# How the weight parts of a ConvGLU up projection lie in SBUF: steps of 8 and 16 elements, or side by side with a shift

## Chip, cores and metric

The kernel runs on one core of one Trainium2 chip. The metric is device time of one execution in microseconds.

## What is computed

One layer of a hybrid encoder block in float32 on 512 tokens of width 1024: an RMSNorm, a wide input projection, three token mixers (a bidirectional mLSTM, a 2-D neighbourhood attention, a cross-attention into 256 memory tokens), a gated merge and an output projection; then a feed-forward network with a convolution and a gate, and a last RMSNorm. Cut to what matters here:

```python
D_MODEL, SEQ, D_FF = 1024, 512, 2816

def conv_glu_ffn(h, w_up, w_conv, b_conv, w_down):
    a, u = jnp.split(h @ w_up, 2, axis=-1)
    return (jax.nn.gelu(dwconv3(a, w_conv, b_conv)) * u) @ w_down

def reference(...):
    h = rms_norm(x, mix_norm_g[l])
    proj = h @ w_in[l]
    ...                      # the three mixers y_ml, y_na, y_xa and their gates
    merged = g_ml * (y_ml @ w_br_ml[l]) + g_na * (y_na @ w_br_na[l]) + g_xa * (y_xa @ w_br_xa[l])
    x = x + merged @ w_out[l]
    x = x + conv_glu_ffn(rms_norm(x, ffn_norm_g[l]), w_ffn_up[l], w_ffn_conv[l], b_ffn_conv[l], w_ffn_down[l])
    return rms_norm(x, final_norm_g)
```

The change is in the product `h @ w_up`. It is 1056 of the kernel's matmuls.

## The kernel before

**Three matmuls for one product.** Each operand is split into a high part of type float32r (a rounded copy) and a low part (the rest). `mm3` (L228 to L231) then issues high x high (L229), high x low (L230) and low x high (L231) into the same PSUM tile. The weights are the stationary operand: each matmul has a weight load of its own (PEld), 128 columns of 128 partitions, and streams 512 tokens past it.

**Weight blocks.** All weights stand in `wflat` in HBM, cut into blocks in the order of use (`BLOCKS`). A block of the up projections, `("ua", f)` for the part that goes through the convolution and `("uu", f)` for the gate, has 8 slices of 128 x 128 (one for each 128 of the 1024 inputs), so 1024 elements on each partition and 24 matmuls. There are 22 tiles f of 128 hidden features, taken in two passes `hh` of 11, and a pass runs `ua 0, uu 0, ua 1, uu 1, ...` and then its half of the down projection (`dn` blocks of 11 slices, 33 matmuls for each of the output tiles).

**From HBM to the array.** `weights(key)` is called when a block is needed. It issues the DMA of blocks up to three ahead (`emit_raw`, L153, three `raw` buffers) and the split of the block one ahead (`emit_split`). The split works in two halves of 4 slices, 512 columns each: ScalarE copies the high part (L213, or L207 where the step is 4), VectorE subtracts for the low part (L214 or L208). Each half goes to a buffer `w` of 1088 elements a partition, of which there are four, so two blocks. A `w` buffer is free again when PE has read it.

**Layouts.** `FORMS` gives for each up block a triple: a step, a shift and a direction; `layout` takes them in turn, 22 of them, so each form is used once in each pass. With step 1, the high part lies at the shift and the low part 512 elements behind it. With step 2, high and low elements alternate, so a weight load reads every second element. With step 4, two slices' high and low elements alternate and a load reads every fourth. Where the direction is 1, `proj` (L360) streams the tokens backwards. All other blocks lie side by side at shift 0.

**The order of work.** The program is written in the order of the model; a scheduler then fixes an order for each engine, and each engine keeps to its own. In the feed-forward part, a tile f needs: the `ua` product in PSUM, the factor `rb2` of the norm, a chain `pad` (L398, VectorE), three taps (L400 ScalarE, L401 and L402 VectorE), the gelu (L1167 ScalarE, L1168 VectorE, L1169 ScalarE, L1170 VectorE), a product with `rb2` on POOL (L1171), the product with the `uu` result (L1174, VectorE) and a split (L235 ScalarE, L236 VectorE) into the hidden activation. For f = 0, `ua` and `uu` are run up to the last slice, then the sums of the norm (L311) go through PE; `ua 1` follows, and only behind it `rstd_row` makes `rb2` (L329 on PE, L331 on ScalarE). PSUM has four banks `mm` for these products.

**Buffers.** The pool `up` has 15 buffers `unit` of 2112 elements a partition. In the feed-forward part, two hold the residual stream, four the normed input, six the hidden activation of a pass.

Of the kernel before, what the change touches and what calls it, by code (L numbers as in the profile page):

```python
# [11 lines left out]
F32 = mybir.dt.float32  # L12
# [5 lines left out]
P = 128  # L18
# [35 lines left out]
def block_list():  # L54
# [50 lines left out]
def hybrid_block(ctx, tc, xT, memT, wflat, vecs, gbias, nabias, outa, outb):  # L105
# [14 lines left out]
    def nm(s):  # L120
        uid[0] += 1
        return f"{s}_{uid[0]}"
# [38 lines left out]
    def layout(key):  # L161

        if key[0] in ("ua", "uu"):
            return FORMS[(2 * key[1] + (key[0] == "uu")) % len(FORMS)]
        return 1, 0, 0

    def form(w, step, at, m, c):

        if step == 2:
            e = w[:, at:at + 2 * m].rearrange("p (j x) -> p x j", x=2)  # L170
            h, l = e[:, 0, :], e[:, 1, :]
        elif step == 4:
            e = w[:, at:at + 2 * m].rearrange("p (y j z x) -> p x y z j", y=2, x=2, z=2)
            h, l = e[:, 0], e[:, 1]
            return h, l, [(h[:, k // 2, k % 2], l[:, k // 2, k % 2]) for k in range(4)]
        else:
            h, l = w[:, at:at + m], w[:, WT - m:] if m > 512 else w[:, 512 + at:512 + at + m]
        q = [slice(k * c, (k + 1) * c) for k in range(m // c)]
        return h, l, [(h[:, s], l[:, s]) for s in q]

# [9 lines left out]
    def emit_split(i):  # L190
        key, n = BLOCKS[i]
        r = raws.pop(i)
        c, hs = halves(i)
        split[i] = []
        for a, b in hs:
            m = (b - a) * c
            if key[0] == "dnl":
                h, l = lastw(4 * key[1] + a, m)
                parts = [(h[:, k * c:(k + 1) * c], l[:, k * c:(k + 1) * c]) for k in range(b - a)]
            else:  # L200
                step, at, _ = layout(key)
                w = wp.tile([P, WT], F32R, tag="w", name=nm("w"), bufs=4)
                h, l, parts = form(w, step, at, m, c)
            for u, v in ((0, P), (P, m)) if i == 0 and a == 0 else ((0, m),):
                src = r[:, a * c + u:a * c + v]
                if len(h.shape) == 4:
                    A.activation(h, src.rearrange("p (y z j) -> p y z j", y=2, z=2), AF.Copy)  # L207
                    V.tensor_tensor(l, src.rearrange("p (y z j) -> p y z j", y=2, z=2), h.bitcast(F32), op=ALU.subtract)  # L208
                    continue
                if i == 0 and a == u == 0:  # L210
                    V.tensor_copy(h[:, u:v], src)
                else:
                    A.activation(h[:, u:v], src, AF.Copy)  # L213
                V.tensor_tensor(l[:, u:v], src, h[:, u:v].bitcast(F32), op=ALU.subtract)  # L214
            split[i].extend(parts)
# [144 lines left out]
    def proj(key, XHs, XLs, n=S, bank=None, at={}):  # L360
        ws = weights(key)
        ps = (bank or mmps)()
        for k in range(KT):
            if layout(key)[2]:
                mm3(ps[:, ::-1], ws[k][0], ws[k][1], XHs[k][:, ::-1], XLs[k][:, ::-1], k == 0, k == KT - 1)
            else:
# [832 lines left out]
def _layout(inp):  # L1199
# [14 lines left out]
    for key, n in BLOCKS:  # L1214
# [39 lines left out]

# [43 lines left out]
```

## Time and profile before

| | |
|---|---|
| median of two runs | 898.5 us (897.97 and 899.04) |
| the profiled execution | 899.35 us |
| its span, first to last instruction | 897.6 us |
| granted TensorE clock, mean | 0.999 |
| PE busy | 888.7 us, 99% |
| PEld (weight loads) busy | 758.9 us, 85% |
| VectorE (DVE) busy | 599.7 us, 67% |
| ScalarE (ACT) busy | 467.6 us, 52% |
| POOL busy | 158.0 us, 18% |
| HBM read | 94.67 MB, 110 GB/s over the span |

PE stands for TensorE's matmuls, PEld for the weight loads, which lie beside matmuls. The profile gives a start and a duration for each instruction; a matmul's end is modelled, so the distance between starts says more than the duration. A row of a group reads: line, engine, operation, output<-inputs, shapes, count | busy us, mean ns of one | idle time of the engine ahead of it, and what ended it. A row of the timeline begins with start and duration in us. The feed-forward part runs from 520.6 us to the end; its first pass of up blocks ends at 644.8, the second runs from 704.66 to 827.50.

### The profile page before, as it was taken

The numbers are of one execution on the slowest core, as the hardware profiler recorded it, in microseconds if no ns is written. First come the engines' busy times: TensorE is split into PE (matmuls) and PEld (weight loads), VectorE is DVE, ScalarE is ACT, GpSimd is POOL, SyncE is SP. The second block draws the span as 40 slices with busy tenths as digits, with TensorE's granted clock in tenths as the row PEclk, the third lists the DMA queues.
The fourth block names the chain that finished last, engine by engine and source line by source line (L and its number), as shares of the span: only waits on it lengthen the run. The fifth ranks groups of instructions, "written<-read, shape, count | busy, mean of one in ns | idle before, by whom it ended". The sixth has DMA issues, their size and how long they took to land.

```text
span 897.6 us, 12396 instructions
## 1 busy us (share of the span) xinstructions
PE 888.7 (99%) x4438; PEld 758.9 (85%) x4438; DVE 599.7 (67%) x1138; ACT 467.6 (52%) x982; POOL 158.0 (18%) x236
## 2 busy tenths in 40 slices
PE   8999999999999999999999999999999999999997
PEld 7899888988888888888888888898888888988897
DVE  6795567747666757998766657677733577777433
ACT  7474446656544647898734435554422344544442
POOL 4201221112070660420000212111100011111010
PEclk9999999999999999999999999999999999999999
DMA  7323633532242443443323432322233322222312
GB/s 251 108 78 131 191 127 118 164 95 94 71 119 94 117 123 125 136 135 118 118 94 106 140 107 80 109 93 95 65 103 96 113 94 95 94 93 89 114 58 94
DMA packets 39437, 99.69 MB, mean 111 GB/s; under 512 B 5960, under 2 KB 13640, under 8 KB 39376
## 3 DMA queue, kind: packets, MB, share of 16 engines
q1 hardware_dynamic: 31728, 92.45, 31.6%
q0 software_dynamic: 7360, 6.32, 3.3%
q8 instruction: 35, 0.57, 0.2%
q14 instruction: 26, 0.21, 0.1%
q10 hardware_dynamic: 288, 0.14, 0.1%
HBM read 94.67 MB, written 4.21 MB: 110 GB/s over the span
## 4 chain that ended last, share of the span: by engine, by line
PE 93%; ACT 2%; DMA 2%; DVE 2%; issue 1%; SPq 0%; POOL 0%; POOLq 0%; ACTq 0%; DVEq 0%
PE mm L229 27%; PE mm L231 27%; PE mm L230 27%; PE at L229 2%; PE at L231 2%; PE at L230 2%; PE at L610 2%; PE at L755 1%; DMA R<-rd 1%; PE at L736 1%; DMA wr<-wflat 1%; DMA rd<-s 0%; PE at L843 0%; ACT s L727 0%; PE at L717 0%
## 5 line engine op out<-in xcount | busy, mean ns | idle before, releaser
L229 PE MATMUL mm<-u,w 128*128 128x512 f32 (+1 forms) x1077 | 418.7, 389 | 1.1 <-ACT w L213 0.8
L230 PE MATMUL mm<-u,w 128*128 128x512 f32 (+1 forms) x1077 | 416.2, 386 | 0.1
L231 PE MATMUL mm<-u,w 128*128 128x512 f32 (+1 forms) x1077 | 416.2, 386 | 0.0
L213 ACT ACTIVATE w<-wr 128x512 fp32r<-128x512 f32 (+1 forms) x290 | 181.9, 631 | 239.1 <-PE mm L231 207.0
L214 DVE TENSOR_TENSOR w<-wr,w 128x512 fp32r<-128x512 f32 (+3 forms) x291 | 220.8, 760 | 116.7 <-ACT w L213 113.4
L231 PEld LDWEIGHTS mm<-u,w 128*128 128x128 f32 x1077 | 207.7, 193 | 39.8 <-DVE w L214 0.4
L229 PEld LDWEIGHTS mm<-u,w 128*128 128x128 f32 x1077 | 207.8, 193 | 39.4 <-ACT w L213 1.3
L230 PEld LDWEIGHTS mm<-u,w 128*128 128x128 f32 x1077 | 207.8, 193 | 38.8 <-DVE u L236 0.8
L1171 POOL TENSOR_TENSOR s<-s,rb 128x512 f32<-128x512 f32 x22 | 30.6, 1392 | 265.2 <-DVE s L1170 256.6
L482 POOL DMA_DIRECT2D u<-nav_d x128 | 62.3, 501 | 73.3 <-PE at L755 33.6
L235 ACT ACTIVATE u<-s 128x512 fp32r<-128x512 f32 x34 | 21.4, 630 | 53.9 <-DVE s L1174 52.2
L236 DVE SCALAR_TENSOR_TENSOR u<-s,u 128x512 fp32r<-128x512 f32 x34 | 23.5, 691 | 14.9 <-ACT u L235 14.7
L598 ACT ACTIVATE E<-R,bi 128x128 f32<-128x128 f32 x80 | 27.9, 395 | 7.8 <-POOL R L579 3.8
L1017 POOL TENSOR_TENSOR acc<-acc,s 128x512 f32<-128x512 f32 x7 | 9.1, 1296 | 128.8 <-ACT s L1016 128.8
L400 ACT ACTIVATE s<-pad,vec 128x512 f32<-128x512 f32 x30 | 24.4, 812 | 6.9 <-DVE pad L398 6.6
L401 DVE SCALAR_TENSOR_TENSOR s<-pad,vec,s 128x512 f32<-128x512 f32 x30 | 22.5, 750 | 3.5 <-ACT s L400 2.6
L229 PE MATMUL mm<-w,u 128*128 128x256 f32 (+1 forms) x80 | 24.7, 308 | 0.0
L1170 DVE SCALAR_TENSOR_TENSOR s<-s,s 128x512 f32<-128x512 f32 x22 | 15.2, 692 | 14.0 <-ACT s L1169 14.0
L231 PE MATMUL mm<-w,u 128*128 128x256 f32 (+1 forms) x80 | 24.4, 305 | 0.0
L230 PE MATMUL mm<-w,u 128*128 128x256 f32 (+1 forms) x80 | 24.3, 304 | 0.0
L402 DVE SCALAR_TENSOR_TENSOR s<-pad,vec,s 128x512 f32<-128x512 f32 x30 | 22.5, 750 | 0.7
L1169 ACT ACTIVATE s<-s 128x512 f32<-128x512 f32 x22 | 13.9, 632 | 17.0 <-DVE s L1168 16.9
(276 smaller groups left out, 1066.7 us busy)
## 6 DMA issues: line engine op xcount, KB each, us to landing
wr<-wflat SPq DMA_DIRECT2D x140, 512.0 KB, 3.4
s<-xT SPq DMA_DIRECT2D x16, 256.0 KB, 4.1
nab<-nabias SPq DMA_DIRECT2D x16, 256.0 KB, 2.7
u<-nav_d POOLq DMA_DIRECT2D x128, 32.0 KB, 2.5
wr<-wflat SPq DMA_DIRECT2D x15, 192.0 KB, 2.4
nav_d<-nv POOLq DMA_DIRECT2D x8, 256.0 KB, 3.5
R<-rd SPq DMA_DIRECT2D x8, 256.0 KB, 3.6
wr<-wflat SPq DMA_DIRECT2D x2, 544.0 KB, 3.4
```

Of the source, the lines that this page charges most:

```text
L213: A.activation(h[:, u:v], src, AF.Copy)
L214: V.tensor_tensor(l[:, u:v], src, h[:, u:v].bitcast(F32), op=ALU.subtract)
L229: PE.matmul(ps, lh, rh, start=start, stop=False)
L230: PE.matmul(ps, lh, rl, start=False, stop=False)
L231: st["mm"] = PE.matmul(ps, ll, rh, start=False, stop=stop).ins
L236: V.scalar_tensor_tensor(l, src, scale, h.bitcast(F32), op0=ALU.mult, op1=ALU.subtract)
L400: A.activation(t1, pad[:, 0:512], AF.Identity, scale=vcol(w, i), bias=vcol(b, i))
L401: V.scalar_tensor_tensor(t1, pad[:, 1:513], vcol(w, n + i), t1, op0=ALU.mult, op1=ALU.add)
L402: V.scalar_tensor_tensor(t1, pad[:, 2:514], vcol(w, 2 * n + i), t1, op0=ALU.mult, op1=ALU.add)
L482: G.dma_start(vw[r * 32:(r + 1) * 32, i * 256:(i + 1) * 256], nav_v[hf, r, CW[b]:CW[b] + 32, hp * 256:(hp + 1) * 256])
L598: A.activation(E[:, i, :], src, AF.Exp, bias=bi[:, d, abs(J - s), s, h:h + 1])
L1171: G.tensor_tensor(c, c, rb2, op=ALU.mult)
```

## The change

`FORMS` now has pairs of a step and a shift: six forms with step 8, six with step 16, ten side by side with shifts of 0, 0, 4, 8, 12, 24, 40, 52, 56 and 60 elements (0 to 240 bytes). Backward tokens, step 2 and step 4 are gone. There are again 22 forms, one for each block of a pass. f = 0 and f = 1 have step 8, f = 2 and f = 3 step 16, f = 4 to 7 and `ua 8` lie side by side, then `uu 8`, `ua 9`, `uu 9`, `ua 10`, `uu 10` have steps 8, 16, 8, 16 and 1.

With step 8, a half block's four slices lie so that element j of the four high parts stands in 4 adjacent words, and element j of the four low parts in the next 4. With step 16, it is the whole block of 8 slices, 8 words and 8 words; such a block is split in one piece (ScalarE 1024 columns, VectorE 1024) and takes a `unit` buffer in place of two `w` buffers. The weights in HBM are put in the same order ahead of time, so a split reads adjacent elements and writes runs of 4 or 8.

```diff
-FORMS = tuple((1, 16 * i, 0) for i in range(4)) + tuple((2, 8 * i, 0) for i in range(8)) + ((4, 0, 0), (4, 16, 0)) \
-    + tuple((1, 16 * i, 1) for i in range(4)) + tuple((2, 16 * i, 1) for i in range(4))
+FORMS = tuple((8, 16 * i) for i in range(4)) + tuple((16, 16 * i) for i in range(4)) \
+    + tuple((1, i) for i in (0, 4, 8, 12, 24, 40, 52, 56, 60)) + ((8, 8), (16, 8), (8, 32), (16, 32), (1, 0))
...
-        k0 = k if n <= HWD else (k + 1) // 2
+        k0 = k if n <= HWD or layout(BLOCKS[i][0])[0] == 16 else (k + 1) // 2
...
     def form(w, step, at, m, c):
-        if step == 2:
-            e = w[:, at:at + 2 * m].rearrange("p (j x) -> p x j", x=2)
-            h, l = e[:, 0, :], e[:, 1, :]
-        elif step == 4:
...
+        if step > 1:
+            g = m // c
+            e = w[:, at:at + step * c].rearrange("p (j x) -> p x j", x=step)
+            h, l = e[:, 0:g], e[:, g:2 * g]
+            return h, l, [(h[:, k], l[:, k]) for k in range(g)]
+        h, l = w[:, at:at + m], w[:, WT - m:] if m > 512 else w[:, 512 + at:512 + at + m]
...
-                w = wp.tile([P, WT], F32R, tag="w", name=nm("w"), bufs=4)
+                w = unit(F32R) if step == 16 else wp.tile([P, WT], F32R, tag="w", name=nm("w"), bufs=4)
...
+                if step > 1:
+                    src, hv, lv = (t.rearrange("p k j -> p j k") for t in (src.rearrange("p (j k) -> p k j", j=c), h, l))
+                    A.activation(hv, src, AF.Copy)
+                    V.tensor_tensor(lv, src, hv.bitcast(F32), op=ALU.subtract)
                     continue
...
-            if layout(key)[2]:
-                mm3(ps[:, ::-1], ws[k][0], ws[k][1], XHs[k][:, ::-1], XLs[k][:, ::-1], k == 0, k == KT - 1)
-            else:
-                mm3(ps[:, :n], ws[k][0], ws[k][1], XHs[k], XLs[k], k == 0, k == KT - 1)
+            mm3(ps[:, :n], ws[k][0], ws[k][1], XHs[k], XLs[k], k == 0, k == KT - 1)
...
+        step = layout(key)[0]
+        if step > 1:
+            g = step // 2
+            b = b.reshape(P, KT // g, g, P).transpose(0, 1, 3, 2)
```

The lines of the feed-forward part move: `mm3` is L231 to L233, the split L209, L210 (steps over 1) and L215, L216, the taps L397 and L399 to L401, the chain's last split L237 and L238.

The order of instructions moves; the prediction speaks of the following place. This is ScalarE before, from the second half of `uu 1`'s split (`w_5498`) to the end of the chain on f = 0 (the last row); `w_5572` and `w_5575` are the two halves of `ua 2`, `rb_5543` is `rb2`, `s_5546` the chain on f = 0, `s_5560` that on f = 1:

```order
L213 ACTIVATE w_5498<-wr_5418 128x512
L213 ACTIVATE w_5572<-wr_5426 128x512
L213 ACTIVATE w_5575<-wr_5426 128x512
L331 ACTIVATE rb_5543<-at_5530 128x512
L400 ACTIVATE s_5546<-pad_138,vec 128x512
L213 ACTIVATE w_5608<-wr_5493 128x512
L1167 ACTIVATE s_5550<-s_5546 128x512
L400 ACTIVATE s_5560<-pad_141,vec 128x512
L1169 ACTIVATE s_5550<-s_5550 128x512
L213 ACTIVATE w_5611<-wr_5493 128x512
L1167 ACTIVATE s_5564<-s_5560 128x512
L235 ACTIVATE u_5412<-s_5546 128x512
```

And ScalarE with the change, the same stretch and three rows more; `u_5572` is the whole block `ua 2`, `u_5605` is `uu 2`:

```order
L209 ACTIVATE w_5498<-wr_5418 128x128x4
L333 ACTIVATE rb_5543<-at_5530 128x512
L399 ACTIVATE s_5546<-pad_138,vec 128x512
L1166 ACTIVATE s_5550<-s_5546 128x512
L399 ACTIVATE s_5560<-pad_141,vec 128x512
L1168 ACTIVATE s_5550<-s_5550 128x512
L1166 ACTIVATE s_5564<-s_5560 128x512
L237 ACTIVATE u_5412<-s_5546 128x512
L209 ACTIVATE u_5572<-wr_5426 128x128x8
L1168 ACTIVATE s_5564<-s_5564 128x512
L209 ACTIVATE u_5605<-wr_5493 128x128x8
```

The split of `ua 2` has moved from ahead of `rb2` to behind the end of the chain on f = 0. VectorE's low part has moved with it. Before, it stood ahead of `pad`:

```order
L214 TENSOR_TENSOR w_5572<-wr_5426,w_5572 128x512
L214 TENSOR_TENSOR w_5575<-wr_5426,w_5575 128x512
L398 TENSOR_TENSOR pad_138<-mm_5434,rb_5543 128x512
L398 TENSOR_TENSOR pad_141<-mm_5501,rb_5543 128x512
L401 SCALAR_TENSOR_TENSOR s_5546<-pad_138,vec,s_5546 128x512
```

With the change, these are the last rows of f = 0's chain on VectorE (its product with `uu 0` in `mm_5435`, a step of f = 1's, its split) and what follows:

```order
L1173 TENSOR_TENSOR s_5546<-mm_5435,s_5546 128x512
L1167 SCALAR_TENSOR_TENSOR s_5564<-s_5564,s_5560 128x512
L238 SCALAR_TENSOR_TENSOR u_5415<-s_5546,u_5412 128x512
L210 TENSOR_TENSOR u_5572<-wr_5426,u_5572 128x128x8
L1169 SCALAR_TENSOR_TENSOR s_5560<-s_5564,s_5560 128x512
```

On PE nothing moves: the first matmul that reads `u_5572` follows the last of `uu 1`, as the first that read `w_5572` did.

More of the change, by code (lines that the diff above doesn't have):

```diff
@@ L85, in block_list, with layout @@
     return L
-FORMS = tuple((1, 16 * i, 0) for i in range(4)) + tuple((2, 8 * i, 0) for i in range(8)) + ((4, 0, 0), (4, 16, 0)) \
-    + tuple((1, 16 * i, 1) for i in range(4)) + tuple((2, 16 * i, 1) for i in range(4))
+FORMS = tuple((8, 16 * i) for i in range(4)) + tuple((16, 16 * i) for i in range(4)) \
+    + tuple((1, i) for i in (0, 4, 8, 12, 24, 40, 52, 56, 60)) + ((8, 8), (16, 8), (8, 32), (16, 32), (1, 0))
+def layout(key):
+    if key[0] in ("ua", "uu"):
+        return FORMS[(2 * key[1] + (key[0] == "uu")) % len(FORMS)]
+    return 1, 0
 BLOCKS = block_list()
@@ L157, in halves @@
         k = n // c
-        k0 = k if n <= HWD else (k + 1) // 2
+        k0 = k if n <= HWD or layout(BLOCKS[i][0])[0] == 16 else (k + 1) // 2
         return c, [(0, k0)] + ([(k0, k)] if k0 < k else [])
[L161 to L165, printed above, removed]
     def form(w, step, at, m, c):
-        if step == 2:
-            e = w[:, at:at + 2 * m].rearrange("p (j x) -> p x j", x=2)
-            h, l = e[:, 0, :], e[:, 1, :]
-        elif step == 4:
-            e = w[:, at:at + 2 * m].rearrange("p (y j z x) -> p x y z j", y=2, x=2, z=2)
-            h, l = e[:, 0], e[:, 1]
-            return h, l, [(h[:, k // 2, k % 2], l[:, k // 2, k % 2]) for k in range(4)]
-        else:
-            h, l = w[:, at:at + m], w[:, WT - m:] if m > 512 else w[:, 512 + at:512 + at + m]
+        if step > 1:
[4 more added lines that the diff above has]
+        h, l = w[:, at:at + m], w[:, WT - m:] if m > 512 else w[:, 512 + at:512 + at + m]
         q = [slice(k * c, (k + 1) * c) for k in range(m // c)]
@@ L196, in emit_split @@
             m = (b - a) * c
+            step = 1
             if key[0] == "dnl":
@@ L200, in emit_split @@
             else:
-                step, at, _ = layout(key)
-                w = wp.tile([P, WT], F32R, tag="w", name=nm("w"), bufs=4)
+                step, at = layout(key)
+                w = unit(F32R) if step == 16 else wp.tile([P, WT], F32R, tag="w", name=nm("w"), bufs=4)
                 h, l, parts = form(w, step, at, m, c)
@@ L363, in proj @@
         for k in range(KT):
-            if layout(key)[2]:
-                mm3(ps[:, ::-1], ws[k][0], ws[k][1], XHs[k][:, ::-1], XLs[k][:, ::-1], k == 0, k == KT - 1)
-            else:
-                mm3(ps[:, :n], ws[k][0], ws[k][1], XHs[k], XLs[k], k == 0, k == KT - 1)
+            mm3(ps[:, :n], ws[k][0], ws[k][1], XHs[k], XLs[k], k == 0, k == KT - 1)
             if k in at:
```

3 lines of the change are left out of this document (removed).

## The prediction, as it was put on record

> **What bounds the kernel now.** I read the page first: the busy shares, then the chain that ended last.
>
> ```profile
> span 897.6 us, 12396 instructions
> PE 888.7 (99%) x4438; PEld 758.9 (85%) x4438; DVE 599.7 (67%) x1138; ACT 467.6 (52%) x982; POOL 158.0 (18%) x236
> PE 93%; ACT 2%; DMA 2%; DVE 2%; issue 1%; SPq 0%; POOL 0%; POOLq 0%; ACTq 0%; DVEq 0%
> ```
>
> TensorE is busy 99% and makes up 93% of the chain. So time changes in two ways only: the distance between the starts of two matmuls (the pitch) changes, or TensorE has to wait. Everything else is cover. Since PE's busy time is modelled, I take the pitch from starts. The next table is the busy time by stretch; I cut the stretches at the first matmuls of weight blocks, so each holds one kind of layout, and a stretch divided by its matmuls (24 to a block) is the pitch.
>
> ```profile
> core 0: us, PE busy (x) PEld busy (x) DVE busy (x) ACT busy (x) POOL busy (x), PEclk, DMA share, GB/s
> 544.08:588.65 44.57, 44.57 (x194) 37.46 (x192) 33.52 (x51) 23.67 (x36) 7.96 (x5) 1.00 0.29 95
> 588.65:600.00 11.35, 11.35 (x49) 11.31 (x49) 8.93 (x12) 5.77 (x9) 1.29 (x1) 1.00 0.30 94
> 600.00:644.80 44.80, 44.80 (x193) 36.77 (x192) 33.10 (x45) 20.67 (x33) 5.52 (x4) 1.00 0.27 81
> 652.30:704.66 52.36, 52.36 (x233) 43.36 (x231) 18.43 (x28) 12.64 (x21) 0.00 (x0) 1.00 0.33 110
> 704.66:710.10 5.44, 5.44 (x26) 4.50 (x24) 2.05 (x3) 1.27 (x2) 0.00 (x0) 1.00 0.30 98
> 710.10:715.70 5.60, 5.60 (x26) 4.51 (x25) 4.15 (x6) 3.17 (x5) 0.00 (x0) 1.00 0.29 94
> 715.70:726.78 11.08, 11.08 (x50) 9.04 (x49) 8.57 (x11) 5.04 (x9) 1.30 (x1) 1.00 0.28 96
> 704.66:827.50 122.84, 122.84 (x529) 103.59 (x528) 91.87 (x120) 57.31 (x87) 13.28 (x10) 1.00 0.28 90
> 868.87:876.79 7.92, 7.92 (x68) 7.92 (x67) 1.70 (x4) 1.86 (x4) 0.00 (x0) 1.00 0.01 2
> 892.00:895.00 3.00, 0.00 (x0) 0.00 (x0) 1.03 (x4) 1.14 (x3) 0.56 (x1) 1.00 0.21 74
> 896.00:897.50 1.50, 0.00 (x0) 0.00 (x0) 0.00 (x0) 0.00 (x0) 0.00 (x0) 0.50 0.00 0
> ```
>
> In the order of the rows: eight blocks with step 2, 44.57 / 192 = 232.1 ns; two with step 4, 11.35 / 48 = 236.5; eight with backward tokens, 44.80 / 192 = 233.3; the down projections, side by side without a shift, 52.36 / 231 = 226.7; one up block side by side at shift 0, 5.44 / 24 = 226.7; one shifted by 64 bytes, 233.3; two shifted by 128 and 192 bytes, 11.08 / 48 = 230.8; then a whole pass of 22 up blocks, 122.84 us. The layouts differ by no more than 10 ns in a pitch of 233.
>
> Weight loads are the other half of it. These are groups by line and shape in four stretches: step 1 (652.4 to 704.5), step 2 (544.1 to 588.3), step 4 (588.5 to 599.7) and the 256-column matmuls (868.9 to 876.7):
>
> ```profile
> L229 PEld LDWEIGHTS mm<-u,w 128*128 128x128 f32 x77 | 14.5, 188 | 3.0
> ...
> L231 PEld LDWEIGHTS mm<-u,w 128*128 128x128 f32 x64 | 12.5, 195 | 2.4
> ...
> L229 PEld LDWEIGHTS mm<-u,w 128*128 128x128 f32 x16 | 5.0, 310 | 0.0
> ...
> L230 PEld LDWEIGHTS mm<-u,u 128*128 128x128 f32 x22 | 4.2, 192 | 0.0
> ```
>
> A load takes 188 ns at step 1, 195 at step 2 and 310 at step 4, and at step 4 no idle time is left ahead of it. That is longer than the pitch, so a part of each load lies beside the next matmul. How much, the 868.87 row tells: the 256-column matmuls run at 7.92 / 66 = 120 ns with loads of 192, so at least 72 ns of a load don't hold up the next one. 310 - 72 = 238, the measured 236.5 within 2 ns: at step 4 the load has just become the limit.
>
> **The change, part by part.** *Pitch.* Each pass gets six blocks with step 8, six with step 16, two side by side at shift 0 and eight shifted. No row shows a load at step 8 or 16. The lower end is that of contiguous weights, 226.7 ns; the upper one is the rise from 195 to 310 ns repeated at each further doubling (the first rival). I take step 4's 236.5: there each element already stands 16 bytes from the last, so what a wider step leaves out is only memory between elements, and it is the nearest row. Then 12 x 24 x 236.5 = 68.1 us, 2 x 24 x 226.7 = 10.9, and 8 x 24 x 232.0 = 44.5 (mean of the rows shifted or with step 2: 61.25 / 264), together 123.5 against 122.8: +0.7 a pass, +1.4 us for both. The shifted blocks' ends, 226.7 and 233.3, move this by -2.0 and +0.5. Backward tokens have no price of their own: 233.3 lies within what shifts cost.
>
> The Trainium skill, SBUF — State Buffer, Specifications (TRN2), gives lines of 16 bytes that need two hits each for full bandwidth. By that rule 4-byte elements lose it at step 4 and nothing more at 8 or 16, which is the choice above; the rise from 195 to 310 ns at step 4 agrees.
>
> *Splits.* ScalarE makes the high part, VectorE the low one. From the groups by line and shape:
>
> ```profile
> L213 ACT ACTIVATE w<-wr 128x512 fp32r<-128x512 f32 x271 | 171.6, 636 | 216.8 <-PE mm L231 189.2 <-DMA wr<-wflat 10.2 <-PE at L231 7.0
> L213 ACT ACTIVATE w<-wr 128x384 fp32r<-128x384 f32 x15 | 7.8, 522 | 19.2 <-PE mm L231 16.3 <-issue 2.8
> L214 DVE TENSOR_TENSOR w<-wr,w 128x512 fp32r<-128x512 f32 x271 | 209.4, 774 | 101.4 <-ACT w L213 98.1
> L214 DVE TENSOR_TENSOR w<-wr,w 128x384 fp32r<-128x384 f32 x15 | 8.4, 557 | 15.4 <-ACT w L213 15.4
> L207 ACT ACTIVATE w<-wr 128x512 fp32r<-128x512 f32 x8 | 9.1, 1133 | 2.2 <-PE mm L231 1.1 <-issue 1.1
> L208 DVE TENSOR_TENSOR w<-wr,w 128x512 fp32r<-128x512 f32 x8 | 10.6, 1320 | 1.9 <-ACT w L207 1.9
> ```
>
> The step-4 split costs 1133 and 1320 ns, the others 636 and 774 (0.69 us in the timeline below). New steps 8 and 16 write runs of 4 or 8 adjacent words, so I price them as contiguous; ends: contiguous and step 4. A half of 512 stays at 0.64 and 0.69 us. A whole block of 1024, at the slope from 384 to 512 columns, is 636 + 4 x 114 = 1.09 us on ScalarE and about 0.69 + 512 x 1 ns = 1.2 us on VectorE, once instead of twice. In a pair of blocks (11.2 us) VectorE is busy about 8.4 us (33.52 of 44.57 in the first row), so neither engine sets the pace; PE is the cover, and these edits cost nothing while splits run ahead of it. ScalarE mostly waits for PE to give a buffer back: 189 of its 217 us idle ahead of L213.
>
> *One split that no longer runs ahead.* Step-16 blocks go whole to a `unit` buffer, and the order of instructions shifts. For f = 2 (the first step-16 block) both halves now stand on ScalarE and VectorE ahead of the chain that works on f = 0; with the change the single split stands behind that chain's last instruction (L235 now, L237 then). PE's order is the same: f = 2 follows `uu` of f = 1. Timeline rows of before around it, the start of the second step-4 block (594.29, for the range further down), and POOL's mean from the page:
>
> ```profile
> 538.88 0.57 ACT L331 ACTIVATE rb<-at 128x512 f32<-128x512 f32 x1
> 539.02 0.69 DVE L214 TENSOR_TENSOR w<-wr,w 128x512 fp32r<-128x512 f32 x1 [1.94 <-ACT w L213]
> 539.63 1.28 DVE L398 TENSOR_TENSOR pad<-mm,rb 128x512 f32<-128x512 f32 x2
> 545.61 1.74 POOL L1171 TENSOR_TENSOR s<-s,rb 128x512 f32<-128x512 f32 x1 [11.99 <-DVE s L1170]
> 548.11 0.63 ACT L235 ACTIVATE u<-s 128x512 fp32r<-128x512 f32 x1 [1.25 <-DVE s L1174]
> ...
> 544.08 0.39 PE L229 MATMUL mm<-u,w 128*128 128x512 f32 x1
> 594.29 0.40 PE L229 MATMUL mm<-u,w 128*128 128x512 f32 x1
> ...
> L1171 POOL TENSOR_TENSOR s<-s,rb 128x512 f32<-128x512 f32 x22 | 30.6, 1392 | 265.2 <-DVE s L1170 256.6
> ```
>
> The split is done at 539.7 and PE needs it at 544.08. The chain on f = 0 can't start before `rb` (538.88 + 0.57), and from there it is one dependence after another over four engines, to 548.74. So with the change the high part is ready at 548.74 + 1.09 = 549.8, and 1.2 us later the low part. The four step-8 blocks ahead (236.5 each) move PE's need by about +0.6 and `rb` by +0.4. First matmul: 550.2 instead of 544.7, a stall of 5.5; its third matmul needs the low part at 551.4, 0.8 us later than the pitch would bring it. With POOL's 1.74 nearer its usual 1.39 it is 0.3 less: **+6.0 us**. If the split took step 4's price (twice 1133 and 1320) it would be +8.5; the low end is 0, were it early after all. What is late next: f = 2's own chain, but PE has four PSUM banks and three blocks to go before it needs one of those, and the split for f = 4 stands behind f = 2's and has over 10 us of cover. In the second pass f = 13 stands behind the chain on f = 11, which isn't held up by `rb`: about 5 us ahead of need, so nothing. A later step-16 split (f = 9, 10, 20, 21) stands a block or more ahead.
>
> *Clock.* The last two rows of the stretch table: PE ends at 891.9, the clock is still full until 895 and half after 896. So an idle stretch of some 4 us halves it, and mine is 5.5. At the start it needed about 4 us of work to come up:
>
> ```profile
> 1.19 3.14 PE L261 MATMUL at<-warm 128*128 128x256 f32 x13 [1.19 <-DVE warm L257]
> ```
>
> 13 matmuls in 3.14 us are 241 ns each, twice the 120 of full speed. Half speed for 3 to 4 us loses 1.6 to 2; bounds 0 and 2, taken 1.6. The Trainium skill, TensorE: Matmul & The Clock Gate, What's actually happening, puts the fall at one idle window of about 3.4 us of a free-running counter; by it 5.5 us may or may not hold a whole window, which would give 0 or 1.7 us.
>
> *Sum.* 1.4 + 6.0 + 1.6 = +9.0 us. The profiled execution took 899.35 us (span 897.6): 908.4. The median of the runs is 898.5, 0.9 lower: **907.5 us**, +1.0%. Its own range is 902 to 912: pitch -1.5 to +2.8 (the shifted blocks' ends, and the two step-4 blocks' 5.64 / 24 = 235.0 and 5.71 / 24 = 238.0, cut at 594.29), stall 5 to 8.5, clock 0 to 2.
>
> **The rivals.** *Slower: the load grows on with the step.* Place: the 12 strided blocks of each pass, 576 matmuls. For it: 188, 195, 310 rise, and the last step left no slack, so each further 10 ns of load cost 5.8 us. Against it: the rise fell at one step, not evenly. Price: 115 ns more per doubling gives loads of 425 and 540 ns, pitches of 353 and 468, 288 x 116.5 + 288 x 231.5 = +100, 1008 us. With half the rise it is pitches of 296 and 353, +51: **958 us**. It decides from a load of 326 ns, 16 x 0.576 = 9 us on top of mine, where 2% is passed. The Trainium skill, Vector Engine (DVE) Microarchitecture Reference, 5.2 Measured stream behaviour on trn2, speaks for it: a write stepping 24 words per element cost VectorE 2.50 ns a column, hops of 4 KiB 1.71, contiguous runs 1.05. My estimate from that page for a load is 188 + 128 x 1.45 = 374 ns, a pitch of 302, 945 us; no run here shows a step over 4 words, and step 4 itself adds (310 - 188) / 128 = 0.95 ns an element.
>
> *No stall.* If f = 2's split runs before the chain all the same, only the pitch is left: 899.9 us. Against it is that each engine keeps its written order.
>
> *A little faster.* Wide steps hide as well as contiguous ones (226.7): -5.6 us on the pitch, 902 with the stall, 894 without; nothing passes 2%, since 1056 matmuls at 226.7 save 6.3 us.
>
> **How the numbers follow.** Forecast 0.50, growing load 0.38, no stall 0.08, a little faster 0.04. The range runs from 898 to 955; above it lies half of the growing load's chance (0.17), below it 0.03. Two per cent, about what a measurement of this kernel can tell from no change, is 880.5 to 916.5: forecast and the two mild cases lie within, so same 0.60, slower 0.39, and 0.01 for a gain that no row shows.
>
> **What would show it.** Right: loads of about 310 ns in step-8 and step-16 stretches, pitch 235 to 240; one PE idle stretch of 5 to 6 us ahead of f = 2's first matmul, released by ScalarE's split, with a half clock or pitches near 470 ns behind it; other stretches as before. Wrong: loads over 326 ns, any PE wait in the second pass's ups, or no gap at f = 2.

## The result, and the profile after

The changed kernel took 910.54 us (median of 910.29 and 910.79), against 898.5 before: a ratio of 1.0134 with a 95% interval of 1.009 to 1.0178. That is slower by 1.3%, inside the 2% that the prediction called no change, and 3.0 us above the 907.5 predicted. The profiled execution took 910.79 us, 11.44 more than the one of before. (Of all executions told of below, one, of the version with every block at shift 0, took 2296 us; it is left out of that version's ratio, and its trace isn't used.) From the page of the changed kernel, the span, TensorE's busy time and the engines' shares of the chain:

```profile
span 909.0 us, 12371 instructions
...
PE 896.5 (99%) x4438; PEld 783.3 (86%) x4438; DVE 589.2 (65%) x1126; ACT 460.0 (51%) x970; POOL 160.5 (18%) x236
...
PE 89%; DMA 3%; issue 3%; ACT 2%; DVE 2%; POOL 1%; SPq 0%; POOLq 0%; DVEq 0%; ACTq 0%
```

TensorE still sets the time: its busy time grew by 7.8 us and its share of the chain fell from 93 to 89%, which fits longer matmuls together with a wait. The busy time by stretch tells them apart. It is cut at the first matmuls of blocks, as before. The rows are the first pass; the second; and in the second pass the four blocks of step 8 that stand together, the four of step 16, shifts of 0 and 16 bytes, six blocks shifted by 32 to 224 bytes, and the one shifted by 240:

```profile
520.35:654.23 133.88, 128.98 (x540) 116.77 (x540) 85.73 (x126) 54.99 (x85) 18.24 (x12) 0.97 0.26 85
...
714.07:839.01 124.94, 124.94 (x530) 114.60 (x530) 84.54 (x114) 53.44 (x81) 14.72 (x10) 1.00 0.27 88
714.07:737.64 23.57, 23.57 (x97) 23.57 (x97) 16.64 (x21) 11.20 (x15) 1.28 (x1) 1.00 0.39 125
737.64:760.42 22.78, 22.78 (x97) 22.74 (x97) 13.68 (x19) 8.01 (x13) 2.96 (x2) 1.00 0.23 79
760.42:771.32 10.90, 10.90 (x49) 9.01 (x48) 6.86 (x10) 4.38 (x8) 1.30 (x1) 1.00 0.14 50
771.32:804.90 33.58, 33.58 (x146) 27.09 (x144) 25.10 (x34) 15.56 (x25) 4.39 (x3) 1.00 0.28 95
804.90:810.37 5.47, 5.47 (x26) 4.56 (x24) 2.88 (x5) 2.14 (x4) 1.68 (x1) 1.00 0.58 187
```

The second pass has no gap and is 124.94 - 122.84 = 2.10 us longer; that is pitch alone. The first pass is 133.88 us; before, from the start of `ua 0` at 520.61 to 644.80, it was 124.19. Of its 9.69 us, I take 2.10 to be the same pitch; 7.59 are left for the gap and the clock. The rest of the kernel is 0.35 us shorter. The pitches, divided as in the prediction: step 8, 23.57 / 96 = 245.5 ns; step 16, 22.78 / 96 = 237.3; shifts 0 and 16 bytes, 227.1; 32 to 224 bytes, 33.58 / 144 = 233.2; 240 bytes, 227.9.

The weight loads by line and shape, first in the step-8 stretch (714.2 to 737.5), then in the step-16 stretch (737.8 to 760.3):

```profile
L232 PEld LDWEIGHTS mm<-u,w 128*128 128x128 f32 x32 | 10.6, 330 | 0.0
...
L232 PEld LDWEIGHTS mm<-u,u 128*128 128x128 f32 x32 | 9.7, 302 | 0.0
```

A load takes 330 ns at step 8 and 302 at step 16, where step 4 took 310. It doesn't grow on with each doubling of the step.

The gap stands where it was predicted, between `uu 1` and `ua 2`. In the timeline (start, duration) the last matmul of `uu 1`, the first of `ua 2` and some that follow, the end of the chain on ScalarE with the split behind it, and VectorE's split:

```profile
545.16 0.40 PE L233 MATMUL mm<-u,w 128*128 128x512 f32 x1
550.43 0.80 PE L231 MATMUL mm<-u,u 128*128 128x512 f32 x1 [4.87 <-ACT u L209]
...
551.69 0.80 PE L233 MATMUL mm<-u,u 128*128 128x512 f32 x1
...
553.14 0.63 PE L233 MATMUL mm<-u,u 128*128 128x512 f32 x1
553.57 0.63 PE L231 MATMUL mm<-u,u 128*128 128x512 f32 x1
...
555.26 0.40 PE L232 MATMUL mm<-u,u 128*128 128x512 f32 x1
555.50 0.40 PE L233 MATMUL mm<-u,u 128*128 128x512 f32 x1
...
548.80 0.63 ACT L237 ACTIVATE u<-s 128x512 fp32r<-128x512 f32 x1 [1.22 <-DVE s L1173]
549.34 1.04 ACT L209 ACTIVATE u<-wr 128x1024 fp32r<-128x1024 f32 x1
...
550.41 1.22 DVE L210 TENSOR_TENSOR u<-wr,u 128x1024 fp32r<-128x1024 f32 x1 [0.26 <-ACT u L209]
```

Read it from the split back: ScalarE splits `ua 2` at 549.34, right behind the last instruction of f = 0's chain; TensorE has its high part at 550.43 and its low part 1.2 us later (550.41 + 1.22 = 551.63). Before 555.26 the matmuls stand about 430 ns apart, behind it about 237. The stretches with the granted clock (third number from the end) show why:

```profile
545.01:548.42 3.41, 0.55 (x3) 0.24 (x1) 2.25 (x4) 1.15 (x2) 1.71 (x1) 1.00 0.00 0
548.42:551.83 3.41, 1.37 (x3) 0.67 (x3) 3.06 (x5) 3.03 (x5) 0.00 (x0) 0.50 0.00 0
551.83:555.24 3.41, 3.41 (x8) 2.71 (x9) 2.23 (x4) 0.96 (x2) 2.20 (x1) 0.50 0.66 208
555.24:558.50 3.26, 3.26 (x15) 3.23 (x14) 2.91 (x5) 2.27 (x4) 0.00 (x0) 1.00 0.61 202
```

The clock is full up to 548.42, half for 6.82 us, and full from 555.24; I have cut that time into two stretches of 3.41 us, for a reason that the second experiment gives. At 550.43 TensorE begins again at half clock.

### The profile page after: what moved, and what is told of

It is laid out like the page before. It is cut to its first block, busy times and chain, and to the rows that moved or that the text cites. A ratio compares the mean times of both kernels' runs of the same rounds, so it can differ in the third digit from the quotient of the medians.

```text
span 909.0 us, 12371 instructions
## 1 busy us (share of the span) xinstructions
PE 896.5 (99%) x4438; PEld 783.3 (86%) x4438; DVE 589.2 (65%) x1126; ACT 460.0 (51%) x970; POOL 160.5 (18%) x236
## 4 chain that ended last, share of the span: by engine, by line
PE 89%; DMA 3%; issue 3%; ACT 2%; DVE 2%; POOL 1%; SPq 0%; POOLq 0%; DVEq 0%; ACTq 0%
PE mm L231 26%; PE mm L233 26%; PE mm L232 26%; DMA s<-xT 3%; PE at L231 2%; PE at L233 2%; PE at L232 2%; PE at L609 2%; PE at L754 1%; PE at L735 1%; DVE u L1009 0%; PE at L842 0%; DVE w L216 0%; ACT s L726 0%; DMA vec<-vecs 0%
## 5 line engine op out<-in xcount | busy, mean ns | idle before, releaser
L231 PE MATMUL mm<-u,w 128*128 128x512 f32 (+1 forms) x981 | 382.2, 390 | 0.3 <-ACT u L237 0.3
L233 PE MATMUL mm<-u,w 128*128 128x512 f32 (+1 forms) x981 | 379.9, 387 | 0.0
L232 PE MATMUL mm<-u,w 128*128 128x512 f32 (+1 forms) x981 | 379.7, 387 | 0.0
L215 ACT ACTIVATE w<-wr 128x512 fp32r<-128x512 f32 (+2 forms) x250 | 154.8, 623 | 214.5 <-PE mm L233 176.0
L216 DVE TENSOR_TENSOR w<-wr,w 128x512 fp32r<-128x512 f32 (+3 forms) x251 | 183.5, 733 | 106.4 <-ACT w L215 104.1
L233 PEld LDWEIGHTS mm<-u,w 128*128 128x128 f32 x981 | 198.6, 202 | 33.2
L232 PEld LDWEIGHTS mm<-u,w 128*128 128x128 f32 x981 | 198.6, 202 | 33.0 <-DVE u L238 0.8
L231 PEld LDWEIGHTS mm<-u,w 128*128 128x128 f32 x981 | 198.6, 202 | 32.9 <-ACT u L237 0.6
L1170 POOL TENSOR_TENSOR s<-s,rb 128x512 f32<-128x512 f32 x22 | 32.8, 1492 | 274.2 <-DVE s L1169 266.1
L231 PE MATMUL mm<-u,u 128*128 128x512 f32 (+1 forms) x140 | 52.5, 375 | 4.9 <-ACT u L209 4.9
L233 PE MATMUL mm<-u,u 128*128 128x512 f32 (+1 forms) x140 | 51.7, 369 | 0.0
L232 PE MATMUL mm<-u,u 128*128 128x512 f32 (+1 forms) x140 | 51.5, 368 | 0.0
L237 ACT ACTIVATE u<-s 128x512 fp32r<-128x512 f32 x34 | 21.4, 630 | 57.1 <-DVE s L1173 55.3
L231 PEld LDWEIGHTS mm<-u,u 128*128 128x128 f32 x140 | 37.5, 268 | 5.4 <-ACT u L209 5.2
L233 PEld LDWEIGHTS mm<-u,u 128*128 128x128 f32 x140 | 37.4, 267 | 1.0 <-DVE u L210 0.7
L232 PEld LDWEIGHTS mm<-u,u 128*128 128x128 f32 x140 | 37.5, 268 | 0.3
L399 ACT ACTIVATE s<-pad,vec 128x512 f32<-128x512 f32 x30 | 24.3, 811 | 17.9 <-DVE pad L397 17.6
L238 DVE SCALAR_TENSOR_TENSOR u<-s,u 128x512 fp32r<-128x512 f32 x34 | 23.4, 689 | 15.0 <-ACT u L237 14.7
L400 DVE SCALAR_TENSOR_TENSOR s<-pad,vec,s 128x512 f32<-128x512 f32 x30 | 22.5, 750 | 8.6 <-ACT s L399 8.5
```

The costliest lines, as they stand in the source:

```text
L231: PE.matmul(ps, lh, rh, start=start, stop=False)
L232: PE.matmul(ps, lh, rl, start=False, stop=False)
L233: st["mm"] = PE.matmul(ps, ll, rh, start=False, stop=stop).ins
L237: A.activation(h, src, AF.Copy, scale=scale)
L238: V.scalar_tensor_tensor(l, src, scale, h.bitcast(F32), op0=ALU.mult, op1=ALU.subtract)
L399: A.activation(t1, pad[:, 0:512], AF.Identity, scale=vcol(w, i), bias=vcol(b, i))
```

## The experiments

Each ratio below is against the kernel before, from runs on the same chip.

**Is the gap the place of the split?** In `weights`, a step-16 block is split one block earlier:

```diff
-        while st["split"] <= min(i + SPLIT_AHEAD, len(BLOCKS) - 1):
+        ahead = i + SPLIT_AHEAD
+        if ahead + 1 < len(BLOCKS) and layout(BLOCKS[ahead + 1][0])[0] == 16:
+            ahead += 1
+        while st["split"] <= min(ahead, len(BLOCKS) - 1):
```

> One edit: a block of step 16 is split two blocks ahead instead of one, so that the split of the third up block's weights (ua 2) stands ahead of the row of reciprocals and the first conv chain on ScalarE and VectorE, not behind them. Theory (the 5.3 us gap before ua 2 and the slow matmuls behind it come only from where this split stands in ScalarE's order): gap and half clock are both gone, the first up pass falls from 133.9 to about 126.3 us (the second pass's 124.9 plus the 1.35 us by which the first was longer before the change), total 910.5 - 7.6 = 902.9 us. Rival (the gap has another cause that stays: the buffer of 2112 words comes free late, or the weights land late): gap still about 5 us, total 909 to 911. Second rival (the split of 1.05 us only pushes the chain back, and TensorE then waits for the chain at the next block): gap of 1 to 3 us one block later, total 904 to 906.

It took 903.63 us, a ratio of 1.0047 (1.0032 to 1.0062). Its two passes:

```profile
519.52:646.30 126.78, 126.77 (x539) 116.04 (x539) 86.06 (x125) 55.08 (x85) 18.56 (x13) 1.00 0.28 92
706.15:831.09 124.94, 124.94 (x530) 114.65 (x530) 85.38 (x114) 53.42 (x81) 14.18 (x10) 1.00 0.27 88
```

The first pass lost 7.1 of its 7.59 us, and the clock stays at 1.00. The second pass, where the change made no gap, is unchanged to 0.01 us. So gap and clock are the price of the split's place in the order of ScalarE and VectorE, as in the first theory; the buffer and the weights' arrival were in time. Most of the 0.5 us that stays is a small case of the second rival: the split of `uu 2` now stands behind the chain on f = 0, and the third matmul of `uu 2` comes 0.4 us late, since its weight load waits for the low part (VectorE's split runs from 549.64 to 550.87; busy time, modelled for matmuls, doesn't show it):

```profile
550.92 0.29 PEld L236 LDWEIGHTS mm<-u,u 128*128 128x128 f32 x1 [0.33 <-DVE u L210]
```

**Is the slow stretch behind the gap the clock?** Matmuls whose result nobody reads fill a part of the gap, first 20, then 38 of them:

```diff
+                if f == 2:
+                    pd = atps()
+                    with tc.issue_after(st["mm"]):
+                        for _ in range(20):
+                            PE.matmul(pd[:, :256], warm[:, :P], warm, start=True, stop=True)
```

> One edit: 20 matmuls of 256 columns on a constant tile, into a bank that nobody reads, stand on TensorE between the last matmul of uu 1 and the first of ua 2, in the 5.3 us in which TensorE now waits for the split. Theory (the idle stretch lowers the granted clock, and the matmuls after it run at half speed until it is back): the gap left behind the 20 is 2 to 3 us, ua 2 runs at about 237 ns once its low part is there instead of 427 ns, its start stays where it is (ScalarE sets that), total 910.5 - 1.7 = 908.8 us. Rival (the 427 ns are waits for the split's other half or for late weights, not clock): pitch stays near 427 ns and the total at 910.5 us.

This expectation failed: 910.73 us (1.0127, 1.0112 to 1.0142), nothing gained. The rival's numbers came, but not for its reason: the clock was half again. In the timeline the 20 matmuls and the first of `ua 2`, with what was left of the gap, and the stretches behind it:

```profile
545.29 2.54 PE L1164 MATMUL at<-warm 128*128 128x256 f32 x20
550.34 0.61 PE L231 MATMUL mm<-u,u 128*128 128x512 f32 x1 [2.51 <-ACT u L209]
...
548.43:551.84 3.41, 1.07 (x3) 0.76 (x4) 3.06 (x5) 3.13 (x5) 0.00 (x0) 1.00 0.00 0
551.84:555.25 3.41, 3.41 (x9) 2.65 (x10) 2.23 (x4) 0.94 (x2) 2.20 (x1) 0.50 0.66 189
```

An idle stretch of 2.5 us still brought half a clock, and it came at 551.84, when TensorE had worked again since 550.34, and lasted 3.41 us. After the change it lasted twice that. A timer that starts when TensorE falls idle doesn't give this: here 4.0 us lie between the end of work and the fall, after the change 2.9 (545.56 to 548.42). A count over fixed stretches of 3.41 us does. Here the stretch from 545.02 to 548.43 held 2.8 us of work, and the clock stayed full behind it. In both traces the stretch up to 551.84 held 1.07 and 1.37 us of work and was followed by half a clock; the one with 3.41 us of work was followed by the full clock. The end of the changed kernel fits the same grid; the clock falls just after 906.80, 105 stretches of 3.413 us after 548.42:

```profile
906.60:906.80 0.20, 0.00 (x0) 0.00 (x0) 0.00 (x0) 0.00 (x0) 0.00 (x0) 1.00 1.11 415
906.80:907.00 0.20, 0.00 (x0) 0.00 (x0) 0.00 (x0) 0.00 (x0) 0.00 (x0) 0.53 1.03 399
```

With 38 matmuls almost no idle time is left:

> As the run with 20 matmuls in the gap before ua 2, but with 38, so that TensorE stands idle for about 0.3 us and not for 2.5 us. Theory (an idle stretch of 2.5 us is enough for the half clock, and it sets in some 3.3 us after the stretch began, even if work has come back): granted clock 1.00 throughout, ua 2 at 237 ns from its third matmul on, uu 2 starts 1.7 us earlier than after the change (556.9 instead of 558.6), total 908.8 us. Rival (the half clock follows from the waits of ua 2 itself or from the split that runs beside it): still 0.50 for 4 us, uu 2 at 558.6, total 910.5 us.

```profile
545.82 4.70 PE L1164 MATMUL at<-warm 128*128 128x256 f32 x38
550.88 0.61 PE L231 MATMUL mm<-u,u 128*128 128x512 f32 x1 [0.37 <-ACT u L209]
...
552.14 0.61 PE L233 MATMUL mm<-u,u 128*128 128x512 f32 x1 [0.42 <-DVE u L210]
...
550.80:554.20 3.40, 2.90 (x10) 2.58 (x11) 2.96 (x3) 2.45 (x4) 1.43 (x1) 1.00 0.28 95
```

Now the clock stays at 1.00. From its start to that of `uu 2`, `ua 2` takes 557.56 - 550.88 = 6.68 us instead of 558.57 - 550.43 = 8.14, so the half clock costs 1.46 us. The time, 909.02 us (1.0112, 1.0097 to 1.0127), is lower by as much, though intervals that overlap can't show that alone. 24 matmuls at 237 ns are 5.69 us, so 1.0 us of `ua 2` is lost otherwise: its third matmul, the first that needs the low part, starts at 552.14, 0.8 us later than the pitch would bring it, and the one behind it follows after 0.45 us in place of 0.24.

**What does a step cost?** Up blocks at steps 2 to 16, all in `unit` buffers, and five blocks of a pass at step 1 (in `form`, high and low parts are `min(4, step)` slices of the stepped view):

```diff
+FORMS = ((1, 0),) * 5 + tuple((s, 0) for s in range(2, 17)) + ((8, 16), (16, 16))
```

> Up blocks at steps 1 to 16, two or four blocks each, all of step 2 and more in the buffers of 2112 words at shift 0; a block of step s uses only min(4, s) of its eight slices, each for several matmuls, so this leaves out the other up weights and its total says nothing; read are the duration of a weight load and the pitch of a matmul at each step. Theory A (step 8 is dear by itself, 32 bytes between elements): load 331 ns and pitch 246 at 8, about 302 to 312 and 235 to 238 at every other step from 4 on, 195 at step 2. Theory B (the dear loads come from the smaller buffers in which the change keeps its step-8 blocks): step 8 here 302 ns and 237, like 16. Theory C (a smooth hump over the step): 6, 7, 9 and 10 lie between, at 315 to 328 ns. Theory D (a cost that goes with the greatest power of two in the step): 6, 10 and 14 like 2 or 4, 12 like 4, odd steps lowest.

Stretches of its second pass, one block of 24 matmuls each, at steps 8, 12 and 16:

```profile
769.02:774.91 5.89, 5.89 (x25) 5.89 (x25) 3.91 (x7) 2.81 (x4) 0.00 (x0) 1.00 0.82 296
...
792.60:799.05 6.45, 6.45 (x25) 6.45 (x25) 3.58 (x5) 2.08 (x3) 0.27 (x1) 1.00 0.00 0
...
816.76:822.37 5.61, 5.61 (x26) 5.61 (x26) 5.12 (x8) 3.98 (x7) 0.00 (x0) 1.00 0.63 210
```

And the loads of this kernel at steps 8 and 12 (one of three lines each):

```profile
L235 PEld LDWEIGHTS mm<-u,u 128*128 128x128 f32 x9 | 3.0, 328 | 0.0
...
L235 PEld LDWEIGHTS mm<-u,u 128*128 128x128 f32 x9 | 3.3, 370 | 0.0
```

To see what a load needs by itself, the same kernel was run with 64 columns in place of 512:

```diff
-            mm3(ps[:, :n], ws[k][0], ws[k][1], XHs[k], XLs[k], k == 0, k == KT - 1)
+            m = 64 if k and key[0] in ("ua", "uu") else n
+            mm3(ps[:, :m], ws[k][0], ws[k][1], XHs[k][:, :m], XLs[k][:, :m], k == 0, k == KT - 1)
```

> The steps 1 to 16 again, each in the large buffers, but from a block's second slice on the matmuls take 64 columns instead of 512 (so the up projections are left unfinished for the other tokens, and the total says nothing): now nothing long runs beside a weight load, and the pitch is what the load itself needs. Theory A (a load has a price of its own by step): pitch 115 at step 1, about 230 to 240 at steps 4 to 7 and 14 to 16, 245 at 8 and 9, 255 at 11 and 13, 268 at 12. Theory B (the load is slowed by the token reads of the matmul that runs beside it): the hump at 8 to 13 is gone, steps 4 to 16 within 10 ns of each other, and all under 230 ns.

All steps of both kernels, in ns. The load is the median of a block's 24 beside 512 columns in the second pass, pitch 512 the block's length over 24, pitch 64 the median distance of starts with 64 columns. In the third line TensorE ran at full clock at steps 1 to 3 (at step 3 for the first five distances) and for most of the blocks shown at 8 and 16, and at half clock at all others:

| step | 1 | 2 | 3 | 4 | 5 | 6 | 7 | 8 | 9 | 10 | 11 | 12 | 13 | 14 | 15 | 16 |
|---|---|---|---|---|---|---|---|---|---|---|---|---|---|---|---|---|
| load | 188 | 193 | 252 | 310 | 304 | 308 | 312 | 328 | 328 | 318 | 345 | 372 | 353 | 328 | 305 | 302 |
| pitch 512 | 227 | 231 | 233 | 236 | 237 | 238 | 238 | 245 | 243 | 241 | 253 | 269 | 256 | 243 | 239 | 234 |
| pitch 64 | 112 | 117 | 176 | 234 | 221 | 222 | 231 | 238 | 238 | 227 | 247 | 269 | 256 | 243 | 230 | 218 |

The load rises to 310 at step 4, stays there to 7, has a first hump at 8 and 9 and a second with its top at 12, and is back at 302 at 16. None of the four theories on the sweep is this curve: 8 is dear also in a `unit` buffer, which ends theory B; 9 and 11 to 13 are dear too, which ends A; C comes nearest but has its top in the wrong place; D fails since odd steps aren't lowest.

The third line shows what the load needs by itself. The hump is still there with 64 columns, 269 at 12 against 218 at 16, so theory B of that run is out and theory A holds in kind (though several steps lie up to 12 ns under its figures): the load has a price of its own by step. The clock has to be minded in reading it. At half clock, steps 2 and 3 both took 213 ns, against 117 and 176 at full clock, so there the load follows the clock; at 8 and 16 it doesn't (last section). At 11 to 14 the pitch beside 512 columns, read at full clock, agrees with the third line within 6 ns, so there the load's own need is the whole pitch. At 4 to 7, 9, 10 and 15 no run gives the load alone at full clock.

At step 8 that is not the whole answer: the load alone needs 238 ns, and the pitch beside 512 columns is 245. So of the 9 ns over the 236.5 taken, the load by itself accounts for about 2; the other 7 show only beside long matmuls, and why is open. A load's recorded duration overstates its need by at least 328 - 245 = 83 ns at step 8 and 372 - 269 = 103 at 12.

**What does step 8 make of the time?** The version with the early split, and all step-8 blocks at step 16:

```diff
-FORMS = tuple((8, 16 * i) for i in range(4)) + tuple((16, 16 * i) for i in range(4)) \
-    + tuple((1, i) for i in (0, 4, 8, 12, 24, 40, 52, 56, 60)) + ((8, 8), (16, 8), (8, 32), (16, 32), (1, 0))
+FORMS = tuple((16, 16 * i) for i in range(4)) + tuple((16, 16 * i) for i in range(4)) \
+    + tuple((1, i) for i in (0, 4, 8, 12, 24, 40, 52, 56, 60)) + ((16, 8), (16, 8), (16, 32), (16, 32), (1, 0))
```

> The version with the early split (no gap before ua 2), and on top of it every block of step 8 at step 16 instead. Theory (the step of 8 is the whole of what the working missed: 12 blocks of 24 matmuls at 246 ns where 236.5 were counted): all strided blocks at 236 to 238 ns, second pass 124.9 - 1.4 = 123.6 us, total 903.6 - 2.7 = 900.9 us, within 2 us of the kernel before the change. Rival (these six blocks of a pass are dear for their place in the pass, or the larger buffers and the undivided splits bring a wait of their own): pitch of the first four blocks stays near 245 ns, or TensorE waits at them for ScalarE; total 902.5 us or more.

It took 901.72 us, a ratio of 1.0027 (1.0018 to 1.0037). Its two passes:

```profile
520.67:646.35 125.68, 125.49 (x540) 114.69 (x539) 79.25 (x118) 50.45 (x77) 16.97 (x12) 1.00 0.25 81
706.20:829.91 123.71, 123.71 (x530) 113.35 (x529) 78.86 (x107) 49.59 (x74) 13.83 (x10) 1.00 0.26 84
```

The second pass is 123.71, 1.23 us less than with step 8 and 0.1 from the 123.6 expected, so the first theory holds there, whatever makes step 8 dear. The first pass gained 1.10; in it TensorE waits 0.2 us at `uu 2` for the low part, the same place as in the version with the early split. The gain of 2.3 us in the two passes is a little under the 2.7 expected, and the time lies 2.6 us over the 899.15 of the kernel before on that chip, not within the 2 expected.

**Why do some shifts cost and others not?** All up blocks lie side by side, at shifts of 0 to 60 elements in turn, and the tokens start 16 elements later in their buffers:

```diff
-    HH = [h2[k // 4][:, (k % 4) * S:(k % 4 + 1) * S] for k in range(KT)]
+    HH = [h2[k // 4][:, 16 + (k % 4) * S:16 + (k % 4 + 1) * S] for k in range(KT)]
```

(`HL` likewise; `FORMS` has the shifts named below.)

> All up blocks side by side, shifts 0, 4, 8 to 60 elements in turn, then 0 and 16 in turn, and the normed tokens, which TensorE reads beside the weight loads, start 16 elements (64 bytes) later in their buffers. Theory (what counts is where the weights lie against the tokens): the pitch of 227 ns stands at shifts 12, 16 and 20, and 231 to 234 ns at all others, 0 among them. Rival (what counts is where the weights lie by themselves): 227 ns at shifts 0, 4 and 60 as after the change, 231 to 234 at the others, 16 among them. Second rival (any place of the tokens off the 256-byte grid costs): no shift is under 231 ns.

Stretches of the second pass: shifts 12, 16 and 20 together; 24; a block at 0; one at 16; then 4 and 8 together:

```profile
719.31:735.66 16.35, 16.35 (x73) 13.52 (x72) 11.74 (x17) 8.11 (x13) 1.80 (x1) 1.00 0.31 97
735.66:741.25 5.59, 5.59 (x25) 4.51 (x24) 3.37 (x5) 1.93 (x4) 1.82 (x1) 1.00 0.27 94
...
813.41:818.90 5.49, 5.49 (x25) 4.51 (x24) 3.37 (x5) 1.94 (x4) 1.81 (x1) 1.00 0.33 97
818.90:824.34 5.44, 5.44 (x25) 4.50 (x24) 4.11 (x7) 3.13 (x5) 0.00 (x0) 1.00 0.19 51
708.12:719.31 11.19, 11.19 (x49) 9.03 (x48) 8.53 (x11) 5.03 (x8) 1.28 (x1) 1.00 0.27 94
```

These are 227.1, 232.9, 228.8, 226.7 and 233.1 ns. The cheap place moved with the tokens, from 60, 0 and 4 to 12, 16 and 20, and 4 became dear: what counts is where the weights lie against the tokens. The theory missed shift 0, which stays at 228.8 and not 231 to 234. That need not speak against the theory. Shift 60 with the tokens at 0 was as cheap as shift 12 with the tokens at 16, so the place seems to repeat every 64 elements; then shift 0 with the tokens at 16 is a difference of 48. The kernel before had that difference too, in a block at shift 48 with the tokens at 0. Its stretch is the first row below, 5.51 / 24 = 229.6 ns, so the two kernels agree; why a difference of 48 is cheaper than most others is open.

```profile
721.27:726.78 5.51, 5.51 (x26) 4.51 (x25) 4.18 (x6) 3.14 (x5) 0.00 (x0) 1.00 0.31 98
...
783.42:789.02 5.60, 5.60 (x26) 4.51 (x25) 3.46 (x6) 1.78 (x4) 1.67 (x1) 1.00 0.27 97
```

The second row is a block of the kernel before at shift 0 with the tokens streamed backwards: 5.60 / 24 = 233.3 ns, where the forward block at shift 0 took 226.7. (The run with the tokens moved was executed once, in 896.16 us; only its pitches are read.)

**All blocks at step 1 and shift 0.** `FORMS = ((1, 0),) * 22`.

> All 44 up blocks side by side at shift 0: no step, no shift. Theory (each part of the cost is a price of a matmul's weight load plus the one stall): 22 blocks of 24 matmuls at 227 ns are 119.9 us in the second pass instead of 124.9, the first pass 121.2 instead of 133.9, total 910.5 - 5.0 - 12.7 = 892.8 us, which is 5.7 us under the kernel before the change. Rival (TensorE was not alone in setting the pace, and ScalarE or VectorE hold it at the old rate): total 896 to 898.5 us, with waits of TensorE for conv chains in the passes.

It took 892.95 us, a ratio of 0.9925 (0.9908 to 0.9942). The kernel was run a second time, for its trace:

> All 44 up blocks side by side at shift 0, a second time, for a trace of an execution at full clock. Theory (TensorE alone sets the pace, each block costs 24 matmuls at 227 ns): every up block at a pitch of 226.7 to 227.7 ns, first pass 121.2, second 119.9 us, total 892.8 us. Rival (the conv chains take over as the bound once TensorE is faster): second pass over 121.5 us with idle stretches of TensorE that end with VectorE or ScalarE.

892.75 us, 0.9932 (0.9915 to 0.9948). Its passes:

```profile
519.12:640.20 121.08, 121.08 (x539) 100.36 (x538) 82.86 (x132) 55.66 (x91) 19.45 (x12) 1.00 0.30 94
700.04:819.72 119.68, 119.68 (x529) 99.10 (x528) 81.68 (x119) 54.62 (x87) 18.11 (x10) 1.00 0.29 92
```

119.68 / 528 = 226.7 ns, with TensorE busy throughout: the sum of pitches is the whole time of the pass, and no other engine takes over. This version is faster than the kernel before and than the changed one.

## Why the prediction was right, and where a term was wrong

- **What bounds it.** TensorE, through pitch and waits alone: the experiments that keep the whole product and were run several times moved the time by what their pitches and gaps say, within 1 us.
- **Stall at f = 2: right.** Predicted +6.0 from the split's new place: 5.2 ahead of the first matmul and 0.8 for the low part. Measured: 550.43 - 545.16 less one pitch of 0.25 is 5.0, and 1.0 is lost inside `ua 2`, 0.8 of it up to the third matmul (the run with 38 matmuls, at full clock). The split took 1.04 and 1.22 us, against 1.09 and 1.2; the contiguous price was the right end. TensorE's need and the split both came later than reckoned (545.4 for 544.7, 549.3 for 548.8), in part because the four step-8 blocks that stand ahead were longer; the difference, which makes the stall, hardly changed.
- **Clock: right in kind, its size in part by luck.** 1.6 taken, 1.46 measured. TensorE worked 4.8 us at half clock (550.43 to 555.24) and not 3 to 4, but for a part of them it would have waited for the low part at any clock. Together with the stall 7.6 predicted, 7.59 measured in the first pass; that they agree to 0.01 is chance. The prediction's reason, that some 4 us of idle time halve the clock, was too strict: 2.5 us did it too. The borders 3.41 us apart agree with what the Trainium skill says in TensorE: Matmul & The Clock Gate, What's actually happening, of a free-running window of about 3.4 us; by it, the idle time needed depends on where the borders fall. The window here didn't have to be idle as a whole: 1.07 us of work in it were too little.
- **Pitch: the term that was too small.** Predicted +1.4 us, at most +2.8, measured 2 x 2.10 = 4.2 (the second pass's, taken twice). The 2.8 us too little are nearly all of the 3.0 that the time lies above the forecast; the time stayed within 902 to 912 because stall and clock, with room of their own, came out near the values taken. The step that failed is "I take step 4's 236.5" for step 8. It holds for step 16 (237.3). At step 8 a pass has 144 matmuls about 9.5 ns dearer, 1.4 us, and exchanging step 8 for 16 took 1.23 of that back. By its own signs, the pitch of 235 to 240 and the loads of about 310 failed at step 8, and one sign of being wrong, a load over 326 ns, showed there.
- **The reason given for it.** The prediction argued that beyond 16 bytes a wider step leaves out only memory between elements. By the rule quoted from the Trainium skill, SBUF — State Buffer, Specifications (TRN2), it is the same answer; the pitches at steps 5 to 7, 15 and 16 agree with 236.5 within 3 ns, and those from 8 to 14 disagree, by 4 ns at 10 and 32 at 12.
- **The rival of a growing load.** Its condition, a load over 326 ns, was met by step 8 with 330, but the price it set on it was not: half the strided blocks were concerned, not all, and 83 to 85 ns of such a load don't hold up the next one, not 72. So it cost 2.7 us and not 9. That the load grows with each doubling is refuted by 302 ns at step 16.
- **Shifts and backward tokens.** The shifted blocks average 231.8 ns, against 232.0 taken. That was right as a mean; it hid two classes, about 227 and 233. That backward tokens have no price of their own doesn't hold at shift 0, where the kernel before took 233.3 backwards and 226.7 forwards; the forecast didn't use it, since the changed kernel's prices came from forward rows.

## What to carry to other kernels

When a buffer's granularity changes, look at where the one larger fill now stands in its engine's order: here one split behind a chain of dependences cost 7.6 us, more than the pitch of all up blocks together (4.2), and issuing it one block earlier gave nearly all of it back. Like durations at two steps (310 ns at 4, 302 at 16) say nothing of the steps between; a sweep with short matmuls beside the loads shows the load's own price at each step, if the clock is looked at for each figure. On this kernel, where TensorE sets the time, weights side by side at shift 0 had the lowest pitch of the layouts that were run, 227 ns.

## What the runs showed that was not expected

- A strided weight load is not monotone in the step: 310 ns at 4, 328 at 8, 318 at 10, 372 at 12, 302 at 16. What makes the humps is open.
- A load at a wide step doesn't follow TensorE's clock, one at a narrow step does. In the run with 64 columns, step 3 had a pitch of 176 ns at full and 213 at half clock (first two rows), step 8 had 238 in both (last two rows; the counts are matmuls that touch the stretch). At step 16 it was 218 at both clocks, at step 2 117 and 213:

```profile
738.15:738.89 0.74, 0.74 (x7) 0.74 (x5) 0.26 (x1) 0.74 (x2) 0.45 (x1) 1.00 0.96 376
738.90:742.00 3.10, 3.10 (x16) 3.10 (x16) 3.10 (x6) 2.48 (x5) 0.00 (x0) 0.50 0.63 188
773.20:776.00 2.80, 2.80 (x13) 2.80 (x13) 0.26 (x1) 0.70 (x1) 1.28 (x1) 1.00 1.01 391
831.50:835.90 4.40, 4.40 (x21) 4.40 (x19) 2.65 (x5) 2.08 (x4) 0.00 (x0) 0.50 0.24 67
```

- The place of the weights against the tokens costs up to 7 ns a matmul: 227 to 228 where they differ by 0 or 4 elements either way, 229 to 230 at 48, and 232 to 234 at most of the other differences run.
- In these traces the clock is decided over fixed stretches of 3.41 us: one with 1.07 us of work led to half a clock, one with 1.37 didn't bring it back, and one with 2.8 kept it full.
